# The norm's sum over partitions: one float32 product against two split products in a one-core decoder trunk

## The chip, the cores and the metric

The kernel runs on one core of one Trainium2 chip. The metric is device time in microseconds (us), from the runs of the whole program. A profile of one execution shows TensorE's products (PE) and weight loads (PEld), VectorE (DVE), ScalarE (ACT), GpSimd (POOL) and the DMA queues; SP is the engine that issues nearly all DMAs here.

## What is computed

Two layers, each a SwiGLU feed-forward block, a mixer and a second feed-forward block, each on a normed input, over 256 positions of width 1024 (feed-forward width 2816). The part that the change touches is the norm.

```python
def rmsnorm(x, g):
    var = jnp.mean(xf * xf, axis=-1, keepdims=True)
    return xf * lax.rsqrt(var + EPS) * g

for l in range(DEPTH):          # DEPTH = 2
    x = x + 0.5 * swiglu_ffn(rmsnorm(x, norm_ffn1[l]), ...)
    x = x + hybrid_mixer(rmsnorm(x, norm_mix[l]), ...)
    x = x + 0.5 * swiglu_ffn(rmsnorm(x, norm_ffn2[l]), ...)
return rmsnorm(x, final_norm)
```

All inputs and outputs are float32.

## The kernel before

**Layout.** The activations are kept transposed: 128 channels of one block on the partitions, the 256 positions along the free axis, eight such blocks for the width of 1024 (`X`, tile XG in the trace). All weights come as one stream of 3152 tiles of 128x128 float32 in the order in which TensorE uses them, by SP's DMA queue in chunks of up to eight tiles into five raw buffers.

**Products of split numbers.** Each float32 weight or activation is split in two parts of type float32r: a high part, which ScalarE makes by copying (line 244), and a low part, which VectorE makes by subtracting the high part from the source (line 245). For weights these are `wh` and `wl`, in a ring of seven chunk buffers each; for activations `XS`, `GA`, `GB` and others. One weight tile is used in three products of 256 columns: high by high, high by low, low by high. `mm` (line 329) issues the three singly (lines 337 to 339, in the mixer's input products); `mm_wide` and `flush` (lines 343 to 376, the feed-forward blocks and the mixer's output) take groups of eight tiles, with one product of 512 columns (line 366, high weight by both parts) and one of 256 (line 363, low weight by the high part) per tile. The order of the two passes alternates from group to group.

**The norm.** The norm's factor is not applied to the input: the products use x times the gain, and the result is multiplied by the factor `rt` when it is taken out of PSUM (`scaled`, line 427, in the mixer; `evac`, line 467, in the feed-forward blocks). So TensorE may begin a block before the factor is known. The squares are made by ScalarE (`sq`, line 401), and VectorE adds them over the eight channel blocks into `acc` (line 403), a 128x256 float32 tile. `norm_r` (line 405) sums `acc` over the partitions by one float32 product with a matrix of ones (line 410), which leaves the sum in every partition; ScalarE takes the root (`sd`), VectorE the reciprocal (`rt`, line 414), and ScalarE loads the table of its next function (`preload`). `norm_r` is called six times: in each of two layers by the first feed-forward block, the mixer, and the second feed-forward block. The very last norm is another function (`last_row`, line 531, product in line 570), which the change leaves alone.

**Where the norm's product stands.** TensorE works strictly in the order written. In a feed-forward block the norm's product is issued behind sixteen tiles (`pairs[:2]`, lines 494 to 499), in the very first block behind forty (line 506). In the mixer the first two PSUM buffers are filled by a loop over half, block k and buffer i, and the product stands behind the twelfth tile, in `if h == 0 and k == 5` (line 648).

**Planner.** `Plan.schedule` (line 125) lists all instructions with estimated durations, keeps TensorE's and the DMA queue's order as written, and orders ScalarE's and VectorE's by a greedy simulation: of what is ready, it takes the instruction with the longest chain of estimated work behind it (`tail`). As TensorE is in order, an instruction that the norm's product waits for has all later products in its tail. The estimate of the old product is 0.43 us, of each new one 0.11.

Of the kernel before, what the change touches and what calls it, by code (L numbers as in the profile page):

```python
# [9 lines left out]
F32R = mybir.dt.float32r  # L10
# [4 lines left out]
S = 256  # L15
# [187 lines left out]
class Trunk:  # L203
# [181 lines left out]
    def prep_x(self, m, gain, key):  # L385

        X, XS = self.X, self.XS
        x = lambda: self.x(m)
        hi = self.act(lambda: XS.t[:, m, 0, :], x, AF.Copy, [(X, m), key], [(XS, (m, 0))], S, scale=gain)
        self.stt(lambda: XS.t[:, m, 1, :], x, gain, lambda: XS.t[:, m, 0, :].bitcast(F32), ALU.mult, ALU.subtract,  # L390
                 [(X, m), (XS, (m, 0)), key], [(XS, (m, 1))], S)
        return hi

    def prep_sq(self, m, add=True, after=()):
        X, A, Q = self.X, self.acc, self.sq
        x = lambda: self.x(m)
        if m == 0:
            self.act(lambda: A.t, x, AF.Square, [(X, m)], [(A, 0)], S, after=after)
        else:
            i = m % 2  # L400
            self.act(lambda: Q.t[:, i, :], x, AF.Square, [(X, m)], [(Q, i)], S, after=after)
            if add:
                self.tt(lambda: A.t, lambda: A.t, lambda: Q.t[:, i, :], ALU.add, [(A, 0), (Q, i)], [(A, 0)], S)

    def norm_r(self, after):

        ps = self.psum()
        A, R, SD = self.acc, self.rt, self.sd
        self.plan.add(
            "PE", 0.43, lambda: self.env.nc.tensor.matmul(ps.t[:, 0, :], lhsT=self.ones.t, rhs=A.t, start=True, stop=True),  # L410
            [(A, 0), (self.ones, 0)], [(ps, 0)])
        o = self.act(lambda: SD.t, lambda: ps.t[:, 0, :], AF.Sqrt, [(ps, 0), (self.eps, 0)], [(SD, 0)], S,
                     scale=1.0 / D, bias=lambda: self.eps.t)
        self.dve(1.67, lambda v: v.reciprocal(out=R.t, in_=SD.t), [(SD, 0)], [(R, 0)])
        self.preload(after, [o])
# [185 lines left out]
    def mixer(self, l, gain):  # L601
# [33 lines left out]
        def win_pair(c):  # L635
            ps = self.psum()
            for h in range(2):
                for k in range(KD):
                    self.xmm(("w_in", l, k, c + h), ps, h, k)
            return ps  # L640


        ps = [self.psum(), self.psum()]
        for h in range(2):
            for k in range(KD):
                for i in range(2):
                    self.xmm(("w_in", l, k, C_POOL + 2 * i + h), ps[i], h, k)
                if h == 0 and k == 5:
                    self.norm_r(AF.Sigmoid)
        for i in range(2):  # L650
            self.scaled(ps[i], UP(2 * i, PADP, UW, 2), [(MB, ("u", 2 * i)), (MB, ("u", 2 * i + 1))])
        for g in range(PG):
# [3 lines left out]
            i = g % 2  # L656
# [91 lines left out]
        def pair(b, h):  # L748
            return lambda: b.t[:, h:h + 2, :]
# [11 lines left out]
        for h in range(0, NH, 2):  # L761
            hh = (h, h + 1)
            for e in hh:
# [10 lines left out]
                out=pair(R, h)(), in0=pair(TT, h)(), scalar1=-1.0, scalar2=1.0, op0=ALU.mult, op1=ALU.add), ts, rs)  # L774
# [7 lines left out]
        for h in range(0, NH, 2):  # L782
# [3 lines left out]
            for e in hh:  # L786
                self.dve(0.34, lambda v, e=e: v.tensor_tensor_scan(
                    out=TT.t[:, e, :], data0=R.t[:, e, :], data1=I.t[:, e, :], initial=0.0, op0=ALU.mult, op1=ALU.add),
# [5 lines left out]
        for i in range(NH // 2):  # L794
            ps = win_pair(C_GELU + 2 * i)
            h = 2 * i
# [16 lines left out]
        ps = [self.psum() for m in range(half)]  # L813
# [5 lines left out]
        def ms(m):  # L819
            b = MS[m // half]  # L820
            return (lambda: b.t[:, m % half, :, :]), (b, (m, 0)), (b, (m, 1))

        for m in range(KD):
# [10 lines left out]
            v, hi, lo = ms(m)  # L834
# [7 lines left out]
        ps = [self.psum(), self.psum()]  # L842
# [47 lines left out]
    def build(self):  # L890
        self.bigs, self.ps, self.raws, self.spl, self.where = {}, [], [], [], []
        self.head = [("L", 0), ("G", 0), ("L", 1), ("G", 1), ("L", 2), ("G", 2), ("L", 3), ("M", 0), ("L", 4), ("G", 3)]
        self.total = DEPTH * (2 * (2 * KF * KD + KD * KF) + 40 * KD + PG + 2 * NH + KD * PG + KD * NH + KD * KD)
        self.X = self.one("XG", [128, KD + KD * S])
        self.XS = Buf(self.plan, lambda: self.env.xsp.tile([128, KD, 2, S], F32R, name="XS"))
        self.prm = self.one("prm", [128, P_COLS])
        self.ones = self.one("ones", [128, 128])
        self.eps = self.one("eps", [128, 1])
        self.dummy = self.one("dummy", [128, 1])
        self.rt = self.one("rt", [128, S])  # L900
        self.sd = self.one("sd", [128, S])
        self.acc = self.one("acc", [128, S])
        self.sq = self.one("sq", [128, 2, S])
        X = self.X

        self.dve(0.15, lambda v: v.memset(self.eps.t, EPS), (), [(self.eps, 0)])
        self.dve(0.15, lambda v: v.memset(self.ones.t, 1.0), (), [(self.ones, 0)])
        self.preload(AF.Silu, ())
        ps = self.psum()
        for _ in range(WARM):  # L910
            self.plan.add(
                "PE", 0.427,
                lambda: self.env.nc.tensor.matmul(ps.t[:, 0, 0:128], lhsT=self.ones.t, rhs=self.ones.t, start=True, stop=True),
                [(self.ones, 0)], [(ps, 0)])

        def load_x(lo, hi, queue="DMA"):
            a = 0 if lo == 0 else KD + lo * S
            self.plan.add(
                queue, (0.37 if queue == "DMA" else 0.3) * (hi - lo),
                lambda: (self.env.nc.sync if queue == "DMA" else self.env.nc.scalar).dma_start(  # L920
                    out=X.t[:, a:KD + hi * S], in_=self.env.xt[:, a:KD + hi * S]),
                (), [(X, m) for m in range(lo, hi)] + ([(X, "g")] if lo == 0 else []))


        load_x(0, 1, "DMA2")
        load_x(1, 2, "DMA2")


        xs = [None, None, None, (2, 4), None, (4, 6), None, (6, 8)]
        for q, runs in enumerate(HEAD):  # L930
            self.chunk(q)
            o = 0
            for n in runs:
                x = xs.pop(0) if xs else None
                if x is not None:
                    load_x(*x)
                self.chunk_run(q, o, n, len(self.where))
                self.runs.append(n)
                o += n
        while len(self.raws) < NRAW:  # L940
            self.more_weights()
        self.dma_in(lambda: self.env.nc.sync.dma_start(out=self.prm.t, in_=self.env.par), 0.4, [(self.prm, 0)])
        his = [self.prep_x(m, lambda m=m: X.t[:, m:m + 1], (X, "g")) for m in range(KD)]
        for m in range(KD):
            self.prep_sq(m, after=[his[min(m + 2, KD - 1)]])
        for l in range(DEPTH):
            c0 = l * P_LAYER
            self.ffn(l, "ffn1_w_up", "ffn1_w_down", c0 + P_NM, l == 0)
            if l == 0:
                self.softplus()  # L950
            self.mixer(l, c0 + P_N2)
            self.ffn(l, "ffn2_w_up", "ffn2_w_down", c0 + P_LAYER + P_N1 if l < DEPTH - 1 else None, False)
        assert len(self.order) == self.total
# [77 lines left out]
```

## Time and profile before

| what | value |
|---|---|
| median of 3 runs | 1091.81 us (1091.4 to 1092.02) |
| profiled execution, its own time | 1091.65 us |
| span of the profiled execution | 1089.9 us |
| PE / PEld / DVE / ACT busy | 99% / 91% / 82% / 66% |
| mean granted TensorE clock | 0.999 of full speed |

The span is from the first to the last instruction; 1.75 us of the execution's own time lie outside it. Busy shares are means over the span. A PE product's record is longer than the step from one product to the next, as products are pipelined, so steps are read from starts.

### The profile page before, as it was taken

The numbers are of one execution on the slowest core, as the hardware profiler recorded it, in microseconds if no ns is written. First come the engines' busy times: TensorE is split into PE (matmuls) and PEld (weight loads), VectorE is DVE, ScalarE is ACT, GpSimd is POOL, SyncE is SP. The second block draws the span as 40 slices with busy tenths as digits, with TensorE's granted clock in tenths as the row PEclk, the third lists the DMA queues.
The fourth block names the chain that finished last, engine by engine and source line by source line (L and its number), as shares of the span: only waits on it lengthen the run. The fifth ranks groups of instructions, "written<-read, shape, count | busy, mean of one in ns | idle before, by whom it ended". The sixth has DMA issues, their size and how long they took to land.

```text
span 1089.9 us, 19566 instructions
## 1 busy us (share of the span) xinstructions
PE 1080.8 (99%) x7276; PEld 993.1 (91%) x7276; DVE 895.4 (82%) x1662; ACT 715.9 (66%) x1408; POOL 0.2 (0%) x4
## 2 busy tenths in 40 slices
PE   9999999999999999999999999999999999999997
PEld 8888889999999888888888888899999998888886
DVE  7999866998988988886688887769989899888763
ACT  8876655669866766665566665655797677666661
POOL 0000000000000000000000000000000000000000
PEclk9999999999999999999999999999999999999999
DMA  8866666656666666666666665666576566666641
GB/s 302 250 210 196 188 197 193 191 180 208 193 192 196 193 194 194 193 193 193 194 193 193 194 194 193 193 187 198 158 230 193 176 193 212 194 194 195 191 138 39
DMA packets 60527, 210.07 MB, mean 193 GB/s; under 512 B 6544, under 2 KB 9232, under 8 KB 60432
## 3 DMA queue, kind: packets, MB, share of 16 engines
q1 hardware_dynamic: 60144, 208.56, 61.7%
q8 instruction: 57, 0.93, 0.4%
q10 hardware_dynamic: 288, 0.27, 0.1%
q14 instruction: 38, 0.31, 0.1%
HBM read 207.75 MB, written 1.05 MB: 192 GB/s over the span
## 4 chain that ended last, share of the span: by engine, by line
PE 98%; DMA 0%; DVE 0%; issue 0%; ACT 0%; SPq 0%; DVEq 0%
PE ps L366 46%; PE ps L363 23%; PE ps L338 10%; PE ps L339 9%; PE ps L337 9%; DMA raw<-in_w 0%; PE ps L544 0%; PE ps L410 0%; PE ps L588 0%; DVE rt L575 0%; PE ps L570 0%; DVE XS L239 0%; SPq L283 0%; ACT sd L225 0%; DVE XF L234 0%
## 5 line engine op out<-in xcount | busy, mean ns | idle before, releaser
L225 ACT ACTIVATE wh<-raw 128x896 fp32r<-128x896 f32 (+3 forms) x672 | 447.0, 700 | 275.2 <-PE ps L366 170.4
L234 DVE TENSOR_TENSOR wl<-raw,wh 128x896 fp32r<-128x896 f32 (+3 forms) x672 | 503.8, 780 | 142.6 <-ACT wh L225 141.0
L366 PE MATMUL ps<-XS,wh 128*128 128x512 f32 x1408 | 334.6, 390 | 0.6 <-DVE XS L239 0.6
L366 PEld LDWEIGHTS ps<-XS,wh 128*128 128x128 f32 x1408 | 257.7, 188 | 48.5 <-ACT wh L225 0.8
L363 PEld LDWEIGHTS ps<-XS,wl 128*128 128x128 f32 x1408 | 174.2, 188 | 8.1 <-DVE wl L234 0.9
L337 PE MATMUL ps<-XS,wh 128*128 128x256 f32 x640 | 177.3, 277 | 0.0
L363 PE MATMUL ps<-XS,wl 128*128 128x256 f32 x1408 | 176.8, 277 | 0.5 <-DVE wl L234 0.4
L339 PE MATMUL ps<-XS,wl 128*128 128x256 f32 x640 | 176.9, 276 | 0.0
L338 PE MATMUL ps<-XS,wh 128*128 128x256 f32 x640 | 176.9, 276 | 0.0
L337 PEld LDWEIGHTS ps<-XS,wh 128*128 128x128 f32 x640 | 120.2, 188 | 0.1
L338 PEld LDWEIGHTS ps<-XS,wh 128*128 128x128 f32 x640 | 120.2, 188 | 0.1
L339 PEld LDWEIGHTS ps<-XS,wl 128*128 128x128 f32 x640 | 120.2, 188 | 0.0
L366 PE MATMUL ps<-GB,wh 128*128 128x512 f32 x341 | 85.1, 390 | 0.0
L366 PE MATMUL ps<-GA,wh 128*128 128x512 f32 x341 | 84.8, 389 | 0.0
L234 DVE TENSOR_TENSOR FT<-ps,FT 128x256 f32<-128x256 f32 x176 | 73.0, 418 | 1.5 <-ACT FT L225 1.5
L366 PEld LDWEIGHTS ps<-GB,wh 128*128 128x128 f32 x341 | 62.5, 188 | 11.6
L366 PEld LDWEIGHTS ps<-GA,wh 128*128 128x128 f32 x341 | 62.3, 188 | 11.5
L225 ACT ACTIVATE FT<-ps 128x256 f32<-128x256 f32 x176 | 64.0, 367 | 5.1 <-DVE FT L234 4.8
L234 DVE TENSOR_TENSOR FT<-FT,rt 128x512 f32<-128x512 f32 x88 | 60.1, 686 | 0.1
L363 PE MATMUL ps<-GB,wl 128*128 128x256 f32 x341 | 46.8, 276 | 0.0
L363 PEld LDWEIGHTS ps<-GB,wl 128*128 128x128 f32 x341 | 44.1, 188 | 1.9
L363 PE MATMUL ps<-GA,wl 128*128 128x256 f32 x341 | 45.7, 276 | 0.0
(126 smaller groups left out, 1159.4 us busy)
## 6 DMA issues: line engine op xcount, KB each, us to landing
raw<-in_w SPq DMA_DIRECT2D x390, 512.0 KB, 4.1
raw<-in_w SPq DMA_DIRECT2D x7, 256.0 KB, 5.2
out<-XF SPq DMA_DIRECT2D x4, 256.0 KB, 2.3
XG<-in_x SPq DMA_DIRECT2D x3, 256.0 KB, 5.0
raw<-in_w SPq DMA_DIRECT2D x2, 128.0 KB, 4.0
XG<-in_x ACTq DMA_DIRECT2D x1, 132.0 KB, 3.7
XG<-in_x ACTq DMA_DIRECT2D x1, 128.0 KB, 4.7
prm<-in_par SPq DMA_DIRECT2D x1, 124.0 KB, 6.1
```

The source lines that it names most:

```text
L225: self.env.nc.scalar.activation(out=out(), in_=in_(), func=func, scale=scale if isinstance(scale, float) else scale(), **kw)
L234: return self.dve(t_dve(n), lambda v: v.tensor_tensor(out=out(), in0=a(), in1=b(), op=op), r, w)
L337: t.matmul(out, lhsT=wh(), rhs=xh(), start=start, stop=False)
L338: t.matmul(out, lhsT=wh(), rhs=xl(), start=False, stop=False)
L339: t.matmul(out, lhsT=wl(), rhs=xh(), start=False, stop=stop)
L363: t.matmul(ps.t[:, 0, :], lhsT=wl(), rhs=x()[:, 0, :], start=first, stop=last, skip_group_check=True)
L366: t.matmul(ps.t, lhsT=wh(), rhs=x(), start=first, stop=last, skip_group_check=True)
```

## The change

The sum `acc` is split like an activation: ScalarE copies it into the high part of a new tile `acc_hl`, VectorE subtracts for the low part, by the existing function

```python
def split(self, hi, lo, src, r, wh, wl, n):
    self.act(hi, src, AF.Copy, r, wh, n)
    self.tt(lo, src, lambda: hi().bitcast(F32), ALU.subtract, tuple(r) + tuple(wh), wl, n)
```

and TensorE sums both parts over the partitions by two float32r products with a float32r copy of the ones, into the same PSUM region. The copy of the ones is made once, at the start, by VectorE. In the mixer the products stand behind sixteen tiles instead of twelve. The feed-forward blocks keep their places.

```diff
--- before.py
+++ after.py
@@ -406,9 +406,13 @@
 
         ps = self.psum()
         A, R, SD = self.acc, self.rt, self.sd
-        self.plan.add(
-            "PE", 0.43, lambda: self.env.nc.tensor.matmul(ps.t[:, 0, :], lhsT=self.ones.t, rhs=A.t, start=True, stop=True),
-            [(A, 0), (self.ones, 0)], [(ps, 0)])
+        hl = self.acc_hl
+        self.split(lambda: hl.t[:, 0, :], lambda: hl.t[:, 1, :], lambda: A.t, [(A, 0)], [(hl, 0)], [(hl, 1)], S)
+        for i in range(2):
+            self.plan.add(
+                "PE", 0.11, lambda i=i: self.env.nc.tensor.matmul(
+                    ps.t[:, 0, :], lhsT=self.ones_r.t, rhs=hl.t[:, i, :], start=i == 0, stop=i == 1),
+                [(hl, i), (self.ones_r, 0)], [(ps, 0)])
         o = self.act(lambda: SD.t, lambda: ps.t[:, 0, :], AF.Sqrt, [(ps, 0), (self.eps, 0)], [(SD, 0)], S,
                      scale=1.0 / D, bias=lambda: self.eps.t)
         self.dve(1.67, lambda v: v.reciprocal(out=R.t, in_=SD.t), [(SD, 0)], [(R, 0)])
@@ -645,7 +649,7 @@
             for k in range(KD):
                 for i in range(2):
                     self.xmm(("w_in", l, k, C_POOL + 2 * i + h), ps[i], h, k)
-                if h == 0 and k == 5:
+                if h == 0 and k == 7:
                     self.norm_r(AF.Sigmoid)
         for i in range(2):
             self.scaled(ps[i], UP(2 * i, PADP, UW, 2), [(MB, ("u", 2 * i)), (MB, ("u", 2 * i + 1))])
@@ -901,10 +905,13 @@
         self.sd = self.one("sd", [128, S])
         self.acc = self.one("acc", [128, S])
         self.sq = self.one("sq", [128, 2, S])
+        self.acc_hl = Buf(self.plan, lambda: self.env.xsp.tile([128, 2, S], F32R, name="acc_hl"))
+        self.ones_r = Buf(self.plan, lambda: self.env.xsp.tile([128, 128], F32R, name="ones_r"))
         X = self.X
 
         self.dve(0.15, lambda v: v.memset(self.eps.t, EPS), (), [(self.eps, 0)])
         self.dve(0.15, lambda v: v.memset(self.ones.t, 1.0), (), [(self.ones, 0)])
+        self.dve(0.2, lambda v: v.tensor_copy(out=self.ones_r.t, in_=self.ones.t), [(self.ones, 0)], [(self.ones_r, 0)])
         self.preload(AF.Silu, ())
         ps = self.psum()
         for _ in range(WARM):
```

## Rows read from the trace of the kernel before

**Rows 1.** The page's first part: busy us, share of the span, instructions of each engine.

```profile
PE 1080.8 (99%) x7276; PEld 993.1 (91%) x7276; DVE 895.4 (82%) x1662; ACT 715.9 (66%) x1408; POOL 0.2 (0%) x4
```

**Rows 2.** The view of waits over the whole span: engine, line, what it waited for: us in total, times, longest. First all of TensorE's, then one of ScalarE's, in which the split of the weights waits for a buffer that TensorE has to leave.

```profile
PE ps L570 <- ACT sq L225: 1.1, 1, 1.1
PE ps L913 <- DVE U L632: 1.0, 1, 1.0
PE ps L366 <- DVE XS L239: 0.6, 1, 0.6
PE ps L363 <- DVE wl L234: 0.4, 1, 0.4
...
ACT wh L225 <- PE ps L366: 170.4, 122, 2.6
```

**Rows 3.** The norm's product by its source line, all six norms: durations in ns (least, median, most), first and last start. PEldq is the queue of TensorE's weight loads.

```profile
L410 PEld LDWEIGHTS ps<-acc,ones x12: 188/188/193, 20.4 to 906.9; 128*128 128x128 f32 x12
L410 PE MATMUL ps<-acc,ones x12: 378/378/382, 20.6 to 907.1; 128*128 128x256 f32 x12
L410 PEldq EVENT_SEMAPHORE  x5: 51/51/51, 190.5 to 905.4; - x5
```

**Rows 4.** Timeline of TensorE at the first mixer: start, duration, engine, line. From the 1st to the 36th of the mixer's products, the norm's two records, and the two products behind them.

```profile
187.00 0.28 PE L337 MATMUL ps<-XS,wh 128*128 128x256 f32 x1
...
190.96 0.28 PE L339 MATMUL ps<-XS,wl 128*128 128x256 f32 x1
191.08 0.59 PE L410 MATMUL ps<-acc,ones 128*128 128x256 f32 x2
191.32 0.47 PE L337 MATMUL ps<-XS,wh 128*128 128x256 f32 x1
191.63 0.28 PE L338 MATMUL ps<-XS,wh 128*128 128x256 f32 x1
```

**Rows 5.** The chain of work that ended last, in order of time (start, us, what), at the norm of the second layer's first feed-forward block.

```profile
549.84 0.43 PE ps L410 x2
```

**Rows 6.** Groups of instructions with shapes kept apart: busy us, mean ns of one | idle before. The first two are the two halves of a split of 128x256, the others the splits of the weights that share these queues.

```profile
L225 ACT ACTIVATE GA<-FT 128x256 fp32r<-128x256 f32 x44 | 17.5, 406 | 2.8 <-DVE FT L234 2.8
L234 DVE TENSOR_TENSOR GA<-FT,GA 128x256 fp32r<-128x256 f32 x44 | 18.3, 417 | 0.0
L225 ACT ACTIVATE wh<-raw 128x896 fp32r<-128x896 f32 x273 | 260.2, 953 | 205.3 <-PE ps L366 157.5 <-issue 30.4 <-ACT wh L225 6.7
L225 ACT ACTIVATE wh<-raw 128x1024 fp32r<-128x1024 f32 x117 | 123.9, 1065 | 69.5 <-PE ps L338 40.6 <-PE ps L366 12.9 <-issue 11.4
L234 DVE TENSOR_TENSOR wl<-raw,wh 128x896 fp32r<-128x896 f32 x273 | 297.4, 1089 | 110.3 <-ACT wh L225 109.1
L234 DVE TENSOR_TENSOR wl<-raw,wh 128x1024 fp32r<-128x1024 f32 x117 | 142.6, 1222 | 31.7 <-ACT wh L225 31.4
```

**Rows 7.** Timeline of VectorE, ScalarE and TensorE at the first mixer's norm, and VectorE and TensorE at the second mixer's; in brackets the idle time before and what ended it.

```profile
189.60 0.42 ACT L225 ACTIVATE sq<-XG 128x256 f32<-128x256 f32 x1 [1.96 <-DVE XG L234]
...
190.05 0.43 DVE L234 TENSOR_TENSOR acc<-acc,sq 128x256 f32<-128x256 f32 x1 [0.48 <-ACT sq L225]
...
192.55 1.75 DVE L414 RECIPROCAL rt<-sd 128x256 f32<-128x256 f32 x1
...
198.20 1.29 DVE L234 TENSOR_TENSOR MB<-ps,rt 128x512 f32<-128x512 f32 x2 [0.17 <-PE ps L339]
...
727.27 0.43 DVE L234 TENSOR_TENSOR acc<-acc,sq 128x256 f32<-128x256 f32 x1 [0.48 <-ACT sq L225]
...
728.30 0.59 PE L410 MATMUL ps<-acc,ones 128*128 128x256 f32 x2
```

**Rows 8.** Timeline at the end: the last square on ScalarE and the product of the final norm that waited for it.

```profile
1083.08 0.31 ACT L225 ACTIVATE sq<-XG 128x128 f32<-128x128 f32 x1 [1.49 <-DVE XG L239]
...
1083.45 0.49 PE L570 MATMUL ps<-sq,ones 128*128 128x128 f32 x2 [1.09 <-ACT sq L225]
```

**Rows 9.** Timeline at the first norm (start of the kernel): VectorE's last two sums into acc, ScalarE's and VectorE's next pieces of the weights' split, the norm's product.

```profile
19.13 0.95 DVE L234 TENSOR_TENSOR acc<-acc,sq 128x256 f32<-128x256 f32 x2
...
20.12 0.94 ACT L225 ACTIVATE wh<-raw 128x896 fp32r<-128x896 f32 x1
...
20.59 0.60 PE L410 MATMUL ps<-acc,ones 128*128 128x256 f32 x2
```

**Rows 10.** Timeline at the norms of the first layer's second feed-forward block, the second layer's first, and the second layer's second: last sum into acc, what stands on VectorE behind it, the norm's product, and in the first of them ScalarE's queue.

```profile
367.18 1.15 ACT L225 ACTIVATE wh<-raw 128x896 fp32r<-128x896 f32 x2 [0.42 <-PE ps L366]
...
367.75 0.42 DVE L234 TENSOR_TENSOR acc<-acc,sq 128x256 f32<-128x256 f32 x1
368.09 1.49 DVE L234 TENSOR_TENSOR wl<-raw,wh 128x128 fp32r<-128x128 f32 x3
...
369.70 0.59 PE L410 MATMUL ps<-acc,ones 128*128 128x256 f32 x2
...
547.17 0.42 DVE L234 TENSOR_TENSOR acc<-acc,sq 128x256 f32<-128x256 f32 x1
...
549.68 0.59 PE L410 MATMUL ps<-acc,ones 128*128 128x256 f32 x2
...
904.97 0.42 DVE L234 TENSOR_TENSOR acc<-acc,sq 128x256 f32<-128x256 f32 x1
...
906.92 0.59 PE L410 MATMUL ps<-acc,ones 128*128 128x256 f32 x2
```

## The prediction

> **What bounds the kernel now.** I read the page's busy shares first: TensorE is busy 99% of the span, VectorE 82%, ScalarE 66% [rows 1]. A high share could still hide waits, so the view of waits came second. It lists everything that TensorE ever waited for between products: 0.6 and 0.4 us while the first operands arrive, 1.0 us for the ones ahead of the warm-up products, 1.1 us in the final norm [rows 2]. Between start and end there is nothing. The reader should see the other direction in the same view: ScalarE, which splits the weights, waited 170.4 us for buffers that TensorE had not yet left [rows 2]. So in the steady part the weights lie split in advance, and time on ScalarE or VectorE is cheap unless TensorE waits for that very result. A change to TensorE's own work counts in full, and so does a wait of TensorE. I therefore looked third at the norm's product and at the moment at which its operand is ready.
>
> **What the change removes: the float32 product.** Its two records last 378 ns each [rows 3], but records overlap, so I take steps. In the first mixer the 1st product starts at 187.00 and the 36th at 190.96, so a step is 3.96 / 35 = 0.113 us. Without the norm, the second product behind the 36th would start at 190.96 + 2 x 0.113 = 191.19; it starts at 191.63 [rows 4]. The norm costs TensorE 0.44 us. The chain gives 0.43 us for it in a feed-forward block [rows 5], so its place does not matter.
>
> **What it adds on TensorE.** Two float32r products of 128x256 with a 128x128 weight, which is the shape of those that step at 0.113 us: 0.23 us. No row shows the ones as a float32r weight; the nearest row is just that step, and the bound from the other side is no gain at all, 0.44. I take the step. The products get two operands to wait for from two engines, where the old one waited for one. Five of the six old ones have a semaphore instruction of 51 ns on the load queue [rows 3]; the one at 190.5, half a microsecond ahead of its product, cost nothing beyond the 0.44 us. Twelve of them exposed would be 0.6 us, which is the bound; I take nothing. TensorE's sum: 6 x (0.44 - 0.23) = **1.3 us less**.
>
> **What it adds in front of the product: a chain.** The old product needed `acc`; the new ones need ScalarE's copy (0.41 us) and then VectorE's subtraction (0.42 us), by the two halves of the same split for `GA` [rows 6]. Hand-overs: a square ends at 190.02 and VectorE's sum starts at 190.05, so 0.03 us [rows 7], taken twice; a square ends at 1083.39 and TensorE's product starts at 1083.45, so 0.06 us [rows 8]. From the end of the last sum into `acc` to the second product the chain is 0.03 + 0.41 + 0.03 + 0.42 + 0.06 = 0.95 us if nothing stands in its way. The second product is due 0.11 us behind the first. Norm by norm:
>
> First norm: the last sum ends at 20.08, the old product starts at 20.59 [rows 9]. The low part reaches TensorE at 21.03, the second product is due at 20.70: 0.33 us late. The planner may also pull the sums forward, since the new chain lengthens what stands behind them; that bounds the loss below by nothing. Above: if ScalarE first does the piece of 0.94 us that it began at 20.12 [rows 9], and VectorE a piece of 1.09 us [rows 6], the loss is 0.33 + 0.94 + 1.09 = 2.4 us. I take 0.33, the direct chain, as the planner puts highest what all later products wait for.
>
> First layer's second feed-forward block: the sum ends at 368.17, the product stands at 369.70, the second due at 369.81; the direct chain ends at 369.12, 0.69 us to spare [rows 10]. But ScalarE is busy until 368.33 and VectorE with three pieces from 368.09 to 369.58 [rows 10], of which the long one takes 1.09 us [rows 6]. If the small and the long piece go first, the subtraction starts at about 369.45 and TensorE gets it at 369.93: 0.1 us late. Bounds: nothing, and 0.95 + 1.09 - 0.69 = 1.35 us with a full piece ahead on both engines. I take 0.1. The second layer's second block has the same distances (905.39 to 906.92) [rows 10]: 0.1 again.
>
> Second layer's first block: 547.59 to 549.68 [rows 10], 1.25 us to spare, more than one long piece. I take nothing; with a piece on both engines it would be 0.8 us.
>
> **What it moves: the mixer's norm, by four tiles.** Four tiles are twelve products, 12 x 0.113 = 1.36 us. The sum ends at 190.48 [rows 7]; at the old place, 191.08 [rows 4], the direct chain would miss the second product (191.19) by 0.24 us. At the new one, 192.44, the second product is due at 192.55 and the chain ends at 191.43: 1.12 us to spare. That covers one piece on ScalarE (1.07) but not one on both engines (1.07 + 1.22 - 1.12 = 1.2 us late) [rows 6]. The second mixer has the same distance, 727.70 to 728.30 [rows 7]. I take nothing for both. What comes later by the move: root, table load and reciprocal. The reciprocal ended at 194.30 and `rt` is first used at 198.20 [rows 7]; 1.36 us later, less the shorter product, leaves over 2.5 us. The root, the table load and the reciprocal change places among the splits, and the full ring covers that. If it were not full, the shift itself, 1.36 - 0.21 = 1.15 us, would be the price in each mixer.
>
> **What it adds elsewhere.** Six copies and six subtractions, 2.4 us on ScalarE and 2.5 us on VectorE over the span. In the steady part the 170.4 us in which ScalarE waited for buffers cover them [rows 2]. At the first norm the rings are not full yet: without that cover a weight's split comes 0.4 us later on each engine, at most 0.8 us; I take nothing, since that wait would run beside the one already counted. The float32r copy of the ones is one small copy on VectorE in the first microseconds, where it idles. No DMA is added or moved, nor anything on GpSimd.
>
> **Sum.** -1.3 + 0.33 + 0.2 = -0.8 us. On the profiled execution's own 1091.65 us that gives 1090.85; the median of the runs is 0.16 us above it, so I forecast 1091.0 us, 0.07% less. I call "the same" what lies within 0.2%, 2.2 us, which is about what a measurement of this kernel can tell.
>
> **A rule against the rows.** The ones' load lasts 188 ns [rows 3], longer than a step; every product of the mixer has a load of the same 128x128 shape before it, and the products still step at 0.113 us [rows 4], so loads are hidden. The Trainium skill, "TensorE: Matmul & The Clock Gate", Part 3, section "The mechanism", says that a weight load overlaps running products only where their row groups differ; all loads here fill all rows. By that rule each new product would show its load as well, and the change would lose on TensorE what the fourth rival below works out. The trace disagrees with it at every one of those 36 steps.
>
> **Rivals.**
>
> 1. *The waits eat the gain.* One norm meets a long piece on both engines, most likely the first, where no buffer is ahead: 2.4 instead of 0.33. Sum -1.3 + 2.4 + 0.2 = +1.3, 1093.1 us. For it: ScalarE started a piece 0.04 us behind the last sum. Against: the planner's order by what stands behind.
>
> 2. *Slower.* The subtraction stands behind a long piece on VectorE, the copy behind one on ScalarE, norm after norm, as ScalarE's and VectorE's queues are fixed beforehand on estimated times, while TensorE waits. At all six: 2.4 + 2 x 1.35 + 0.8 + 2 x 1.2 = 8.3, net +7.0. It decides from 3.5 us of waits on (1.3 + 2.2), which the first norm and one mixer reach: 3.6, net +2.3, 1094.1 us. Against: it takes wrong orders at two places at least, and the old product, with the same queues in front, never waited [rows 2].
>
> 3. *Faster by more than 0.2%.* The new products give at most 1.3 us; 0.9 more must come from a luckier order at the start, where TensorE's two waits for operands are 1.0 us together [rows 2]. Then -2.3: 1089.5 us. Nothing in the diff points there.
>
> 4. *The products gain nothing.* If each cost its step and its load, 0.113 + 0.188 = 0.30, a norm would cost 0.60 against 0.44: +1.0 instead of -1.3, and with the waits 1093.3 us. If only the rate fell to the old one's, the sum would be +0.5, 1092.3 us. Against: the steps of rows 4.
>
> **Numbers.** Forecast (1090.3 to 1091.8, the waits between nothing and 1.3): 0.70. Rival 1: 0.17. Rival 2: 0.07. Rival 3: 0.03. Rival 4: 0.03, of which 0.01 by loads. Faster is rival 3, 0.03; slower is rival 2, 0.07; the same is the rest, 0.90. The range leaves out most of rivals 2 and 3 and the far end of the first: 1090.1 to 1093.0 us.
>
> **What the changed profile would show.** Two products per norm at 0.113 us each, the chain's share of them about 0.23 instead of 0.43. Waits of TensorE on VectorE for the low part of `acc_hl`: about 0.3 us at the first norm, at most 0.1 at the second blocks, none in the mixers. The last stretch, from the last block's end, as before. I am wrong if a wait of a microsecond stands at a norm, if new waits appear between norms because the planner's order moved, or if the float32r products step more slowly than the weights'.

## The result: 1% slower, in the two mixers

The changed kernel took 1102.51 us (median of 4 runs, 1102.47 to 1102.74), the kernel before in the same comparison 1091.74. The ratio is 1.010, with an interval of 1.0088 to 1.0112: 10.8 us more, where 0.8 less was forecast. The range, 1090.1 to 1093.0, missed it.

First the page's parts one and two for the changed kernel, busy shares and the granted clock; the first line answers to [rows 1].

```profile
PE 1092.3 (99%) x7276; PEld 1004.6 (91%) x7276; DVE 900.4 (82%) x1669; ACT 717.3 (65%) x1414; POOL 0.2 (0%) x4
...
PEclk9999999999999999999999999999999999999999
```

TensorE has as many instructions as before and 11.5 us more busy time. It does not wait more. All waits of its products, which answer to [rows 2] (the one that is new on its load queue is of 0.2 us, at the first norm, and comes up again below):

```profile
PE ps L574 <- ACT sq L225: 1.1, 1, 1.1
PE ps L920 <- DVE eps L912: 1.0, 1, 1.0
PE ps L363 <- DVE wl L234: 0.2, 1, 0.2
```

So neither the chain in front of the norm nor a new order of the planner took the time: the products themselves take longer. Busy time per stretch shows where. These are two stretches of 100 us inside the two mixers: start and end, length, TensorE's busy time and number of products, granted clock, share and rate of DMA. The kernel before:

```profile
200.00:300.00 100.00, 100.00 (x885) 1.00 0.64 194
750.00:850.00 100.00, 100.00 (x884) 1.00 0.63 193
```

The changed kernel:

```profile
200.00:300.00 100.00, 100.00 (x851) 1.00 0.60 187
750.00:850.00 100.00, 100.00 (x851) 1.00 0.60 188
```

The engine is busy all the time at full granted clock in both, and does 33 or 34 products fewer in 100 us. Now the timeline of TensorE at the first mixer's norm in the changed kernel, which answers to [rows 4]:

```profile
192.02 0.28 PE L337 MATMUL ps<-XS,wh 128*128 128x256 f32 x1
192.13 0.28 PE L338 MATMUL ps<-XS,wh 128*128 128x256 f32 x1
192.24 0.28 PE L339 MATMUL ps<-XS,wl 128*128 128x256 f32 x1
192.36 0.40 PE L413 MATMUL ps<-acc_hl,ones_r 128*128 128x256 f32 x2
192.59 0.28 PE L337 MATMUL ps<-XS,wh 128*128 128x256 f32 x1
192.71 0.28 PE L338 MATMUL ps<-XS,wh 128*128 128x256 f32 x1
192.83 0.28 PE L339 MATMUL ps<-XS,wl 128*128 128x256 f32 x1
192.95 0.28 PE L337 MATMUL ps<-XS,wh 128*128 128x256 f32 x1
193.06 0.28 PE L338 MATMUL ps<-XS,wh 128*128 128x256 f32 x1
193.18 0.28 PE L339 MATMUL ps<-XS,wl 128*128 128x256 f32 x1
```

Ahead of the norm the starts are 0.113 apart. Behind it they are 0.118 apart, with the same shapes, the same operands and no gap. The chain of work shows how long this lasts. For the changed kernel, the norm, the first product behind it, and the first products of the next block:

```profile
192.52 0.24 PE ps L413 x2
192.76 0.12 PE ps L337
...
348.22 0.94 PE ps L363 x8
349.17 3.65 PE ps L366 x16
352.82 1.81 PE ps L363 x16
```

For the kernel before, the 24th product ahead of the next block, and that block's first eight:

```profile
339.94 0.11 PE ps L337
...
342.66 0.91 PE ps L363 x8
```

Behind the norm the changed mixer has 440 tiles, 1320 products: (348.22 - 192.76) / 1320 = 0.1178 us each. In the kernel before a step at the mixer's end takes (342.66 - 339.94) / 24 = 0.1133 us. The slow step holds through the whole stage; the next eight products of 256 columns still take 0.94 us where the chain of before has 0.91 for eight, and behind sixteen of 512 columns the step is 1.81 / 16 = 0.113 again. Two mixers: 2 x 1320 x 0.00445 (the difference before rounding) = 11.7 us. The shorter products give back about 1.2 us of this. By the starts of the products, the feed-forward blocks take about 0.3 us more than where the step stays fast (the first run below): some 0.06 us behind each mixer's end and behind each of their norms but the first. Together that is the 10.8.

### The profile page after: what moved, and what is told of

Same layout as the page of the kernel before. It is cut to its first block, busy times and chain, and to the rows that moved or that the text cites. A ratio compares the mean times of both kernels' runs of the same rounds, so it can differ in the third digit from the quotient of the medians.

```text
span 1100.7 us, 19572 instructions
## 1 busy us (share of the span) xinstructions
PE 1092.3 (99%) x7276; PEld 1004.6 (91%) x7276; DVE 900.4 (82%) x1669; ACT 717.3 (65%) x1414; POOL 0.2 (0%) x4
## 4 chain that ended last, share of the span: by engine, by line
PE 98%; DMA 0%; DVE 0%; ACT 0%; issue 0%; DVEq 0%; SPq 0%
PE ps L366 46%; PE ps L363 23%; PE ps L338 10%; PE ps L339 10%; PE ps L337 10%; DMA raw<-in_w 0%; PE ps L548 0%; PE ps L592 0%; PE ps L413 0%; ACT wh L225 0%; DVE rt L579 0%; PE ps L574 0%; DVE XS L239 0%; ACT sd L225 0%; DVE wl L234 0%
## 5 line engine op out<-in xcount | busy, mean ns | idle before, releaser
L337 PE MATMUL ps<-XS,wh 128*128 128x256 f32 x640 | 179.7, 281 | 0.0
L338 PE MATMUL ps<-XS,wh 128*128 128x256 f32 x640 | 179.7, 281 | 0.0
L366 PEld LDWEIGHTS ps<-GA,wh 128*128 128x128 f32 x341 | 62.3, 188 | 11.5
```

Source lines behind the costliest of these rows:

```text
L337: t.matmul(out, lhsT=wh(), rhs=xh(), start=start, stop=False)
L338: t.matmul(out, lhsT=wh(), rhs=xl(), start=False, stop=False)
L366: t.matmul(ps.t, lhsT=wh(), rhs=x(), start=first, stop=last, skip_group_check=True)
```

## The experiments

**What was to be explained.** Each product has a weight load of its own, and the load for the next product starts with the product: at 192.02 us the changed kernel starts the product of line 337 (above) and the load for line 338. The loads of the ones start the same way, beside the last product ahead of the norm and beside the first of the pair:

```profile
192.02 0.19 PEld L338 LDWEIGHTS ps<-XS,wh 128*128 128x128 f32 x1
...
192.25 0.30 PEld L413 LDWEIGHTS ps<-acc_hl,ones_r 128*128 128x128 f32 x2
```

So each step is a load and a product side by side: the load reads the stationary operand (the weights), the product streams the other operand. Something at the norm makes each later step 4.5 ns longer. The code holds a hint that I had read past: `chunk_run` (lines 289 to 297) puts the split weights, with one exception, not at the start of their buffers but 16 columns (`LINE`, 64 bytes) or 64 columns (`SPARE`, 256 bytes) in, by stage and part. By the addresses in the built program, which no trace shows, XS, the split sum and the new ones all begin at a multiple of 256 bytes along their partition, and the mixers' weights 64 bytes behind one. Theory A: the place of the ones decides. Theory B: any such pair of products does it. Theory C: the new place behind sixteen tiles does it.

### The ones moved by 64 bytes

```diff
-        self.ones_r = Buf(self.plan, lambda: self.env.xsp.tile([128, 128], F32R, name="ones_r"))
+        self.ones_r = Buf(self.plan, lambda: self.env.xsp.tile([128, 128 + SPARE], F32R, name="ones_r")[:, LINE:LINE + 128])
```

> The changed kernel with the float32r ones moved 64 bytes along their partition (16 columns, the constant LINE by which the mixer's weights are moved too). In the changed kernel the step from product to product in the mixers is 0.1178 us from the norm on, where it was 0.1133 before; 1320 products per mixer x 0.0045 x 2 = 11.9 us, which is the whole loss. Theory A (the place of the ones in SBUF decides: a weight load that begins at the wrong offset beside a product of 256 columns shifts loads against products, and the shift stays): the step is 0.113 after the norm and the time 1102.5 - 11.9 = 1090.6 us, about 1.2 below the kernel before. Theory B (any pair of float32r products on the sum leaves this step, wherever the ones lie): 1102.5 us, step 0.118. Theory C (the place behind sixteen tiles does it): 1102.5 us.

Measured: 1090.24 us (10 runs, 1090.02 to 1090.59) against 1091.61 for the kernel before, ratio 0.9987, interval 0.9978 to 0.9997. It is the fastest of all kernels tried, 1.4 us below the kernel before. The timeline of TensorE at the first mixer's norm:

```profile
191.91 0.28 PE L339 MATMUL ps<-XS,wl 128*128 128x256 f32 x1
192.03 0.39 PE L413 MATMUL ps<-acc_hl,ones_r 128*128 128x256 f32 x2
192.25 0.28 PE L337 MATMUL ps<-XS,wh 128*128 128x256 f32 x1
192.37 0.28 PE L338 MATMUL ps<-XS,wh 128*128 128x256 f32 x1
192.48 0.28 PE L339 MATMUL ps<-XS,wl 128*128 128x256 f32 x1
192.59 0.28 PE L337 MATMUL ps<-XS,wh 128*128 128x256 f32 x1
```

The pair costs 192.25 - 192.03 = 0.22 us and the step stays 0.113. Theories B and C fall: place and pair are unchanged here.

### The sum moved instead, and both moved

```diff
-        self.acc_hl = Buf(self.plan, lambda: self.env.xsp.tile([128, 2, S], F32R, name="acc_hl"))
+        self.acc_hl = Buf(self.plan, lambda: self.env.xsp.tile([128, 2 * S + SPARE], F32R, name="acc_hl")[:, LINE:LINE + 2 * S].rearrange("p (a t) -> p a t", t=S))
```

> The changed kernel with the split sum acc_hl moved 64 bytes along its partition and the ones where the change put them. Theory A in the form that only the weights' own offset counts: 1102.5 us, step 0.118. Theory A in the form that the distance between the weights being loaded and the operand being streamed counts: the second load of the ones no longer lies as the streamed sum does, but the mixer's first weights behind the norm do; a shift of the step at the norm in one place or the other, and a time that is either 1090.6 or 1102.5 us. Theories B and C: 1102.5 us.

Measured: 1102.37 us, step 0.118. That is the number of the first form of theory A, but the second allows it too: here the first load of the ones still stands beside XS at an equal place, and the mixer's first weights, 64 bytes off, are loaded beside the sum, now 64 bytes off. Moving both tells the two forms apart (A1 and A2 in the next expectation).

> The changed kernel with both the ones and the split sum moved 64 bytes. Theory A1 (what counts is where the loaded weights lie by themselves: at 64 past a multiple of 128 bytes a load is harmless): 1090.2 us, step 0.1133. Theory A2 (what counts is the distance between the weights being loaded and the operand being streamed meanwhile, and equal places modulo 128 bytes are bad): the ones and then the mixer's weights are loaded beside the sum at the same place, so the step is 0.118 behind the norm and the time 1102.4 us.

Measured: 1102.64 us, step 0.118. The ones lie where they were harmless in the first experiment, yet the slow step is there once the sum lies there too. So the place of the ones by itself does not decide, and A1 falls. Theory A2, the distance between the weights that are being loaded and the operand that is being streamed, fits all runs. It is not the only rule that does: that loads want an offset of 64 bytes and streamed operands one of 0, each for itself, would give the same times, and no run separates the two.

### Other distances

> The changed kernel with the ones moved by 128 bytes instead of 64. If the place counts modulo 128 bytes (A1 and A2): as the changed kernel, 1102.4 us, step 0.118. If any move away from the allocation that the change made would do (theory D): 1090.2 us.

> The changed kernel with the ones moved by 32 bytes. If 64 bytes are the unit, so that 32 stays beside the streamed operand: 1102.4 us, step 0.118. If a smaller move is enough: 1090.2 us.

The edits are the first one with 32 and with 8 columns in place of `LINE`. Measured: 1102.55 us for 128 bytes, 1102.62 for 32. The tile of the ones is as large here as in the first experiment, so everything behind it lies as it lay there, and only the place of the ones differs between the fast run and the two slow ones. With the sum at 0, the ones are harmful at 0, 32 and 128 bytes and harmless at 64, of the four places that were tried.

### The kernel before with the mixers' weights at multiples of 256 bytes

```diff
-            h = LINE if kind == "narrow" or (kind == "low" and a == 0) else SPARE
-            e = 0 if kind == "high" and a == 0 else LINE
+            h = LINE if kind == "low" and a == 0 else SPARE
+            e = 0 if kind == "narrow" or (kind == "high" and a == 0) else LINE
```

> The kernel before, its float32 norm product included, with the mixer's weights (both parts) put at multiples of 256 bytes, as XS and the other streamed operands are, instead of 64 past them. Theories A1 and A2: the step of the mixers is 0.118 from their first products on, without any new norm product: 2 x 1368 products x 0.0045 = 12.3, 1103.9 us, or more if a load that is always misplaced costs more than one that was misplaced once. If the slow step belongs to the norm's two products (theory B): 1091.6 us, step 0.1133.

Measured: 1110.41 us, ratio 1.0172, 18.9 us slower than the kernel before, with its old norm. TensorE's products in the two stretches:

```profile
200.00:300.00 100.00, 100.00 (x835) 1.00 0.59 185
750.00:850.00 100.00, 100.00 (x836) 1.00 0.60 185
```

The step is 0.120 from the mixers' first products on (160.01 us for the 1332 behind the norm, by the starts): 2 x 1368 x 0.0068 = 18.6 us. The other 0.3 us lie in the last row, whose weights are of the same kind (`narrow`) and move too. So the effect needs none of the new products. I had expected 0.118; loads that are all misplaced cost half as much again as one that was misplaced once.

### The place behind sixteen tiles, and behind twelve

```diff
-                if h == 0 and k == 5:
+                if h == 0 and k == 7:
```

> The kernel before with its float32 product moved behind sixteen tiles in the mixers, nothing else. Theory C (the place): about 1103 us, step 0.118 behind the norm. Theories A and B (the new products): as the kernel before, 1091.7 us within 0.3, step 0.113.

Measured: 1091.61 us against 1091.61, ratio 0.9999 (0.9989 to 1.0009). The move by itself costs nothing, its `rt` comes early enough.

> The changed kernel with its products back behind twelve tiles in the mixers. Theory C: step 0.113, and TensorE waits about 0.24 us or more for the low part in each mixer: 1090.6 + 0.5 = 1091.1 us. Theories A and B: step 0.118 from the norm on, over 12 products more per mixer, and the same wait: about 1103 us. If a wait of TensorE for the low part should reset the step, 1091.1 us here would tell that too, and TensorE's view of waits would show it.

Measured: the ten runs fall apart into 1091.1 (two), 1096.8 to 1097.5 (seven) and 1103.5 (one). The steps of 6 us are those of one mixer. The profiled run, 1096.93 us, had one mixer at each step:

```profile
200.00:300.00 100.00, 100.00 (x885) 1.00 0.62 193
750.00:850.00 100.00, 100.00 (x852) 1.00 0.61 186
```

In both mixers TensorE stood still at the norm. The first mixer's two norm products and the product behind them:

```profile
190.55 0.75 PE L413 MATMUL ps<-acc_hl,ones_r 128*128 128x256 f32 x2
191.13 0.28 PE L337 MATMUL ps<-XS,wh 128*128 128x256 f32 x1
```

The pair took 191.13 - 190.55 = 0.58 us, two steps and 0.35 us of waiting for the low part; in the second mixer it took the same. In the first mixer the step came back to 0.113 within five products, in the second it did not. So with a wait of that size in the pair the slow step does not always last. What decides was not found, nor whether the wait ends the slow step or keeps it from starting.

### A float32 product behind the new pair

```diff
+        if after == AF.Sigmoid:
+            self.plan.add(
+                "PE", 0.43, lambda: self.env.nc.tensor.matmul(
+                    ps.t[:, 1, :], lhsT=self.ones.t, rhs=A.t, start=True, stop=True), [(A, 0), (self.ones, 0)], [(ps, 1)])
```

> The changed kernel with the old float32 product issued in each mixer right behind the two new ones, its result unused. Theory S (the slow step is a state that the misplaced loads start and that stays by itself though the later loads are well placed; behind the float32 product of the kernel before the step came back to 0.113 after some five products, so it ends the state): 1102.5 - 11.8 + 2 x 0.44 = 1091.6 us, step 0.1133. Theory T (something that stays changed in the kernel, such as the addresses behind the two new tiles, slows every later product): 1102.5 + 0.9 = 1103.4 us, step 0.118.

Measured: 1091.46 us (1091.1 to 1091.55) against 1091.57. Doing more work, 0.44 us per mixer, takes 11 us off the changed kernel. The timeline at the first mixer:

```profile
192.15 0.40 PE L413 MATMUL ps<-acc_hl,ones_r 128*128 128x256 f32 x2
192.39 0.59 PE L418 MATMUL ps<-acc,ones 128*128 128x256 f32 x2
192.63 0.47 PE L337 MATMUL ps<-XS,wh 128*128 128x256 f32 x1
192.94 0.28 PE L338 MATMUL ps<-XS,wh 128*128 128x256 f32 x1
193.07 0.28 PE L339 MATMUL ps<-XS,wl 128*128 128x256 f32 x1
193.18 0.28 PE L337 MATMUL ps<-XS,wh 128*128 128x256 f32 x1
193.30 0.28 PE L338 MATMUL ps<-XS,wh 128*128 128x256 f32 x1
193.41 0.28 PE L339 MATMUL ps<-XS,wl 128*128 128x256 f32 x1
```

The pair is misplaced as in the changed kernel, all SBUF addresses are the same, and from the third product behind the float32 one on the step is 0.113 again. Theory S holds and theory T falls: the slow step is a state. Misplaced loads start it, well placed loads of the same width keep it, and one float32 product, or sixteen of 512 columns, end it.

## Why the prediction was wrong, point by point

**TensorE's own sum** was right for what it counted. With the ones well placed, the pair costs 0.22 us where I took 0.23, and the time is 1.37 us below the kernel before where the products' term was 1.3.

**"the nearest row is just that step"**: here the prediction failed. I priced the new product by the shape of others, and took the step of the products behind it as given, so that a change of that step stood in the sum at nothing. The step of 0.113 is not a property of the shape: it depends on where loaded and streamed operands lie, for which the kernel places its weights by stage. The two new tiles came without such a place. The missing term is 1320 products x 0.00445 us in each of two mixers, 11.7 us in all, nine times the gain. The pair itself took the 0.23 us that I had for it (192.36 to 192.59), so none of the three signs of being wrong that I had written down names what happened. The bound that I gave ("no gain at all, 0.44") was a bound on the norm's own time, and nothing in the sum could grow behind it.

**A faint sign stood in the trace of before.** TensorE's timeline there goes on behind the last of [rows 4]:

```profile
191.75 0.28 PE L339 MATMUL ps<-XS,wl 128*128 128x256 f32 x1
191.86 0.29 PE L337 MATMUL ps<-XS,wh 128*128 128x256 f32 x1
191.99 0.28 PE L338 MATMUL ps<-XS,wh 128*128 128x256 f32 x1
192.10 0.28 PE L339 MATMUL ps<-XS,wl 128*128 128x256 f32 x1
192.22 0.28 PE L337 MATMUL ps<-XS,wh 128*128 128x256 f32 x1
```

From the start at 191.63 [rows 4] the steps are 0.12, 0.11, 0.13, 0.11 and 0.12 before they settle. I stopped reading one row too early and booked the whole disturbance as the norm's 0.44 us. The five steps are only some 0.02 us too long together; they show that the step behind a norm product can change, not for how long it may.

**The chain in front of the product.** First norm: I took 0.33 us late, with the planner possibly pulling the sums forward. It did. The rows that answer to [rows 9]:

```profile
18.04 0.96 DVE L234 TENSOR_TENSOR acc<-acc,sq 128x256 f32<-128x256 f32 x2
...
19.14 0.40 ACT L225 ACTIVATE acc_hl<-acc 128x256 fp32r<-128x256 f32 x1
19.27 1.09 DVE L234 TENSOR_TENSOR wl<-raw,wh 128x896 fp32r<-128x896 f32 x1 [0.27 <-ACT wh L225]
...
20.28 0.42 DVE L234 TENSOR_TENSOR acc_hl<-acc,acc_hl 128x256 fp32r<-128x256 f32 x1
20.59 0.54 PE L413 MATMUL ps<-acc_hl,ones_r 128*128 128x256 f32 x2
```

The sum ended at 19.00 instead of 20.08, and the subtraction, behind one long piece on VectorE, at 20.70; the view of waits of the norm's line has 0.2 us for it, on the load of the second product. In the second blocks I took 0.1 us each; no wait shows there. In the mixers I took none, and there is none. Behind twelve tiles I had 0.24 us; measured 0.35.

**The rivals.** Rival 2 had the sign and not the cause: no wait for the split was behind it. Rival 4 said that the new products might step more slowly, and priced only themselves. My chance of 0.07 for slower was worked out from waits alone.

**The weighed rule** on loads and row groups does not hold here as it was put: loads of 188 ns overlap products in every step, slow or fast. The Trainium skill, "TensorE: Matmul & The Clock Gate", Part 3, section "The mechanism", also names a load into the background weight buffer as a case in which a load is pulled ahead of running products, which the prediction left out; the traces show the overlap and not the buffer. Another sentence of the same page would have misled as well. The Trainium skill, "TensorE: Matmul & The Clock Gate", section "Step-by-step: what each phase is for", says that TensorE reads weights and streamed operand by separate ports, so that a load takes no read bandwidth from a running product. Whoever concludes from it that the place of a load cannot matter is contradicted here for products of 256 columns: the same loads go with steps of 0.113 or 0.120 us by where they lie. Whether read bandwidth is what is lost, no run shows.

## What to carry to other kernels

Where a weight load stands beside every product, the address of every stationary operand can count, a small constant's too: here, beside products of 256 columns, a new weight tile did no harm 64 bytes from the operand streamed beside its load, and harm at 0, 32 and 128. This is no rule for other widths: beside products of 512 columns this kernel loads nearly all its weights from multiples of 256 bytes, as XS lies, and sixteen still take 3.65 us, 0.228 us each, about two steps of 256 columns. Give a new operand the same offset as the tuned ones next to it, and read the step between starts on both sides of any inserted product: one misplaced pair of 0.23 us cost 5.9 us in each mixer. When busy time grows at an unchanged instruction count, full clock and no waits, look at the step first.

## What the runs showed of the hardware

- TensorE ran the same stream of 256-column products with a load each at two lasting steps, 0.1133 and 0.1178 us, at a granted clock of 1.00 in both. With the mixers' weights at multiples of 256 bytes, as the streamed operands are, a third step was seen, 0.120.
- The slow step outlived its cause by 1320 products, and ended behind one float32 product of 256 columns, behind sixteen products of 512, and in one of two mixers it did not last behind a pair with a wait of about 0.35 us.
- That loads and streamed operands collide when SBUF is read is an explanation that fits all places tried; no run shows the collision itself, nor why well placed loads keep the slow step.
